# Gate and up of an FFN column tile as one 2x2 block product with seven products for eight

## The chip, the cores and the metric

The kernel runs on one core of a Trainium2 chip. The metric is the device time of one execution in microseconds; the median of three runs is given. The engines are TensorE (PE, and PEld for its weight loads), VectorE (DVE), ScalarE (ACT), GpSimd (POOL) and SyncE (SP), which issues most transfers.

## What is computed

One decoder layer, on 512 prompt tokens and 8 x 4 sample tokens together (T = 544 columns), in float32. Only the two FFNs change; they are the macaron half steps before and after the mixing part:

```
def swiglu(x, w_gate, w_up, w_down):
    return (jax.nn.silu(x @ w_gate) * (x @ w_up)) @ w_down

# per layer, D_MODEL = 1024, D_FF = 2816
x = x + 0.5 * SwiGLU_1(RMSNorm(x))
h = RMSNorm(x); z = h @ w_in          # seven groups of columns
x = x + concat(MoBA(q_a, k_a, v_a), gate * norm(HGRN2(q_b, f_b, i_b))) @ w_out
x = x + 0.5 * SwiGLU_2(RMSNorm(x))
```

## The kernel before

Activations lie feature-major: 8 tiles of 128 features by 544 tokens, and a product is taken in two halves of 272 tokens. Float32 accuracy comes from a split of each operand into two float32r parts, hi and lo; one k tile of a product is three matmuls, hi x hi, hi x lo and lo x hi (`gemm_unit`). ACT makes the high part of a weight (a cast, `whi`), DVE the low one (`wlo` = raw - hi). The moving operands are `xh`, `xl` for the input of an FFN and `hh`, `hl` for its hidden features.

Each FFN has 22 column tiles of 128 hidden features, in groups of 8, 8 and 6 (`FGROUPS`). For each tile `gemm` makes the gate product and then the up product, each of 8 k tiles in two halves, so 96 matmuls of 272 columns. `hidden` evacuates them: gate x R (R is 1/rms per token) into `t_g`, Silu into `t_s`, times R, and up x `t_s` into `t_h`, which is split into `hh` and `hl`. After a group come its eight down products (`ffn`), each of 48 matmuls (36 in the last group), which are added to x.

A weight block is 8 k tiles by 128 columns (512 KB). `w_dma` loads it on SP's queue into one of two raw buffers, `w_split` splits it into one of two pairs `whi`, `wlo`; `next_w` takes a block and starts the split and the load of later ones.

The order of all instructions comes from a planner. `Order.run` steps a backbone of products and several side chains (norms, attention, the recurrence, loads of tables); `Engine.cost` estimates each instruction, and `give_out` writes the instructions out sorted by estimated start. On each engine they then run in that order, so an instruction that waits holds back all behind it. PSUM has eight banks, three of them (`NMM`) for the products, named `mm`.

The planner's estimate of a float32r matmul, and the call that this change replaces for most tiles, are these lines:

```
            if args[1].dtype == F32R:
                self.order.columns = n * rows
                return n / 2400.0 + OVER
...
                yield from self.gemm(xg, KD, gate, both=f == 0)
                yield from self.gemm(xg, KD, up)
```

Of the kernel before, what the change touches and what calls it, by code (L numbers as in the profile page):

```python
# [50 lines left out]
OVER, TICK, WARM_COLUMNS = 0.0027, 3.413, 3060  # L51
# [42 lines left out]
class Root:  # L94
    """A tile that is allocated when the first instruction that uses it is given out."""
# [10 lines left out]
class View:  # L106
    """A view of such a tile; model has the same shape."""
# [30 lines left out]
class Rows:  # L138
    """Row indices of an indirect load."""
# [36 lines left out]
class Engine:  # L176
    """Passes instructions on and keeps an estimate of when each of them runs."""
# [65 lines left out]
class Order:  # L243
    """Writes down the steps of several dependent chains between the units of a backbone of matrix
    products, in the order in which they are expected to be ready, and gives the instructions out
    in the order in which they are expected to start."""
# [40 lines left out]

    def fit(self, part, s, cost):
        """the first time from s on at which the engine is free for so long"""
# [91 lines left out]
class Core:  # L381
    """The engines, each behind an estimate of its time."""
# [9 lines left out]
class Build:  # L392
# [31 lines left out]
    # ---- weights: [nk*128, 128] blocks, each split exactly into two float32r parts, loaded ahead  # L424
    def weight_blocks(self):
        a, out = self.a, []

        def block(m, nk, r0, c0):
            out.append((m[128 * r0:128 * (r0 + nk), c0:c0 + 128].rearrange("(k p) m -> p k m", p=128), nk))

        def ffn(p):
            for g0, ng in FGROUPS:
                for f in range(g0, g0 + ng):
                    block(a[p + "_gate"][0], KD, 0, 128 * f)
                    block(a[p + "_up"][0], KD, 0, 128 * f)
                for m in range(KD):
                    block(a[p + "_down"][0], ng, g0, 128 * m)

        ffn("ffn1")
        for n, j in IN_ORDER:  # L440
            block(a["w_in"][0], KD, 0, COLS[n] + 128 * j)
        for m in range(KD):
            block(a["w_out"][0], KD, 0, 128 * m)
        ffn("ffn2")
        return out

    def w_dma(self):
        if self.w_loaded < len(self.blocks):
            src, nk = self.blocks[self.w_loaded]
            raw = self.tl(self.wp, [128, 8, 128], "raw", bufs=2)  # L450
            self.nc.sync.dma_start(raw[:, :nk], src)
            self.w_raw.append((raw, nk))
            self.w_loaded += 1

    def w_split(self):
        if self.w_raw:
            nc = self.nc
            raw, nk = self.w_raw.pop(0)
            hi = self.tl(self.wp, [128, 8, 128], "whi", F32R, bufs=2)
            lo = self.tl(self.wp, [128, 8, 128], "wlo", F32R, bufs=2)  # L460
            nc.scalar.copy(hi[:, :nk], raw[:, :nk])
            nc.vector.tensor_tensor(lo[:, :nk], raw[:, :nk], hi[:, :nk].bitcast(F32), op=ALU.subtract)
            self.w_ready.append((hi, lo))

    def first_weights(self):
        """the first block, loaded and split by halves: returns it and the steps that load and split"""
        nc = self.nc
        src, nk = self.blocks[self.w_loaded]
        self.w_loaded += 1
        raw = self.tl(self.wp, [128, 8, 128], "raw", bufs=2)  # L470
        hi = self.tl(self.wp, [128, 8, 128], "whi", F32R, bufs=2)
        lo = self.tl(self.wp, [128, 8, 128], "wlo", F32R, bufs=2)
        parts = [slice(i, i + nk // 2) for i in (0, nk // 2)]

        def load(i):
            nc.sync.dma_start(raw[:, parts[i]], src[:, parts[i]])

        def split(i):
            k = parts[i]
            nc.scalar.copy(hi[:, k], raw[:, k])  # L480
            nc.vector.tensor_tensor(lo[:, k], raw[:, k], hi[:, k].bitcast(F32), op=ALU.subtract)

        return (hi, lo), load, split

    def next_w(self, ahead=True):
        if not self.w_ready:
            self.w_split()
            self.w_dma()
        w = self.w_ready.pop(0)
        if ahead and not self.w_ready:  # L490
            self.w_split()
        if len(self.w_raw) < 2:
            self.w_dma()
        return w

    def gemm_unit(self, ps, h, w, k, x, first, last):
        nc = self.nc
        (hi, lo), (xh, xl) = w, x
        for i, (ww, xx) in enumerate(((hi, xh), (hi, xl), (lo, xh))):
            nc.tensor.matmul(ps[:, :HT], ww[:, k], xx[:, self.cols(h)], start=first and i == 0, stop=last and i == 2)  # L500

    def gemm(self, x, nk, evac, order=None, both=False):
        """a product by halves of the tokens, each evacuated when it is done;
        both: the halves side by side, for operands that are just being made"""
        w = self.next_w()
        ks = list(order or range(nk))
        ps = []
        for hh in ((0, 1),) if both else ((0,), (1,)):
# [5 lines left out]
            for n, k in enumerate(ks):  # L514
                for h in hh:
                    self.gemm_unit(ps[h], h, w, k, x[k], n == 0, n == nk - 1)
# [5 lines left out]
            if self.have_R():  # L522
                self.flush()

# [21 lines left out]
    # ---- 1/sqrt(mean + eps) on a small tile  # L546
# [17 lines left out]
    def norm_add(self, m, x):  # L564
        """adds the squares of feature tile m of x to the running sum"""
# [9 lines left out]
    def norm(self):  # L575
        """chain: R = 1/rms per token, over all partitions"""
# [24 lines left out]
    def hidden(self, pool, i, hs):  # L601
        """evacuations of gate and up of one tile of hidden features: silu(gate) * up, split"""
# [12 lines left out]
        def up(p, h):  # L615
            c = self.cols(h)
            nc.vector.tensor_tensor(u[:, c], p, s[:, c], op=ALU.mult)
            if h:
                hi = self.tl(pool, [128, T], f"hh{i}", F32R)
                lo = self.tl(pool, [128, T], f"hl{i}", F32R)  # L620
                nc.scalar.copy(hi, u)
                nc.vector.tensor_tensor(lo, u, hi.bitcast(F32), op=ALU.subtract)
                hs[i] = hi, lo
# [3 lines left out]
    # ---- SwiGLU half step; x: list of feature-major tiles updated in place  # L627
    def ffn(self, pool, x, xg, done, first=None):
        nc = self.nc
        for g0, ng in FGROUPS:  # L630
            hs = {}
            for f in range(g0, g0 + ng):
                gate, up = self.hidden(pool, f - g0, hs)
# [7 lines left out]
            yield from self.settle()  # L641
            for m in range(KD):
# [29 lines left out]
    def small(self, rp):  # L672
        """chain: loads and tables for the middle part, spread over time"""
# [34 lines left out]
        self.rs = rp.tile([HEADS, RLEN], F32, name="rsb")  # L708
# [8 lines left out]
    def small_setup(self):  # L717
        nc = self.nc
        nc.vector.tensor_copy(self.lm, self.lmi)
        # lower bound lb -> (1 - lb) / 2, its complement and its negative  # L720
# [13 lines left out]
        # page table -> row-group indices of every (batch, quarter)  # L734
# [4 lines left out]
        # relative bias per distance, reversed: r[h, y] = bias of distance RTOP - y  # L739
        for c0 in range(0, RLEN, 512):  # L740
# [3 lines left out]
            nc.vector.tensor_copy(self.rs[:, c0:c0 + n], p[:HEADS, :n])  # L744
        rd = self.dp.tile([HEADS, RLEN], F32, name="rbias")
        nc.sync.dma_start(rd, self.rs)
        # one row per query offset, so that skewed reads have a positive step
# [8 lines left out]
    def load_x(self, pool, p, x):  # L756
        """x by column chunks, turned feature-major and split as they come"""
# [15 lines left out]
        self.blocks = self.weight_blocks()  # L773
        self.w_loaded, self.w_raw, self.w_ready = 0, [], []
# [55 lines left out]
        for n in range(KD + LAG):  # L830
# [10 lines left out]
            for m in range(2):  # L841
                k = n - LAG * m
                if 0 <= k < KD:
                    for h in range(2):
                        self.gemm_unit(ps[m][h], h, w[m][0], k, xg[k], k == 0, k == KD - 1)
                if n == 4 and m == 0:
                    self.w_dma()
                    self.w_dma()
                if n == KD - 1 and m == 0:
                    self.w_split()  # L850
# [4 lines left out]
        self.w_split()  # L855
        self.w_dma()
        self.w_dma()
        return xg, out

    def ffn1(self, xspill):  # L860
        nc = self.nc
        with self.pool("ffn1") as pool, self.pool("relb") as rp:
# [6 lines left out]
            out = []  # L869

# [5 lines left out]
            yield from self.ffn(pool, x, xg, done, first)  # L876
# [21 lines left out]
    def stack(self, dst, src, i):  # L898
        """src [NS, 128] split in two parts: the high one twice, the low one as block 1 + i of dst"""
# [10 lines left out]
    def to_tokens(self, z, dst, dst_s):  # L910
        """feature-major [128, T] -> dst [128 tok, 4, 128] and dst_s [NS, 128], or stacked parts of it"""
# [711 lines left out]
```

## Time and profile before

| | |
|---|---|
| Time, median of 3 runs (lowest, highest) | 1244.88 us (1244.19, 1245.5) |
| Span of the profiled execution | 1246.9 us |
| PE busy | 1223.8 us, 98% |
| DVE busy | 672.2 us, 54% |
| ACT busy | 406.5 us, 33% |
| POOL busy | 127.8 us, 10% |
| Mean DMA rate | 116 GB/s |

The profiled execution is shown by its span alone, from its first to its last instruction, 2.0 us above the median of the three runs. The first FFN runs to about 430 us, the mixing part from there to about 800 us, the second FFN from about 843 us to the end. A busy PE says little of itself, since matmuls overlap; what the parts of an FFN cost is read from the number of matmuls in a stretch.

### The profile page before, as it was taken

What the parts mean: (1) busy time and instruction counts of PE and PEld (TensorE: products, weight loads), DVE (VectorE), ACT (ScalarE), POOL (GpSimd) and SP (SyncE); (2) the same over time, 40 slices, a digit from 0 to 9 for tenths busy, and PEclk for the clock granted to TensorE, in tenths of its full rate; (3) what the DMA queues carried; (4) which work ended last, traced back from release to release, by engine and by line L of the source; (5) the groups of instructions that cost most, each with busy time, mean ns of one, the idle gap of its engine ahead of it and who ended that gap; (6) DMA issues with size and microseconds to landing.
All of it is one profiled execution on the core that took longest, in us unless ns stands there. A gap on an engine that the chain in (4) does not pass through costs nothing.

```text
span 1246.9 us, 25516 instructions
## 1 busy us (share of the span) xinstructions
PE 1223.8 (98%) x10979; PEld 1161.4 (93%) x10979; DVE 672.2 (54%) x1309; ACT 406.5 (33%) x685; POOL 127.8 (10%) x143
## 2 busy tenths in 40 slices
PE   8999999999999999999999999899999999999998
PEld 7999999999999998988878876799999999999998
DVE  5544434443445678888667557655443344433443
ACT  5322222221223325555445423332221122212222
POOL 3000000000000231001233244120000000000000
PEclk8999999999999999999999999999999999999999
DMA  5333343323233552332665786332223232332333
GB/s 143 88 87 94 113 144 95 92 86 85 85 92 97 181 179 71 103 91 72 188 188 172 230 270 225 128 96 86 85 85 101 84 88 85 86 94 84 92 87 88
DMA packets 213476, 144.68 MB, mean 116 GB/s; under 512 B 9299, under 2 KB 201323, under 8 KB 213364
## 3 DMA queue, kind: packets, MB, share of 16 engines
q1 hardware_dynamic: 202836, 106.59, 29.4%
q0 software_dynamic: 10432, 36.32, 8.8%
q8 instruction: 87, 1.43, 0.5%
q14 instruction: 25, 0.20, 0.1%
q10 hardware_dynamic: 96, 0.14, 0.0%
HBM read 133.94 MB, written 11.83 MB: 117 GB/s over the span
## 4 chain that ended last, share of the span: by engine, by line
PE 92%; DVE 3%; DMA 2%; ACT 2%; issue 1%; SPq 0%; ACTq 0%
PE mm L273 78%; PE sm L273 15%; DMA raw<-ffn_gate 2%; DVE wlo L273 1%; ACT whi L273 0%; ACT sq L273 0%; DVE sc L273 0%; DVE sst L273 0%; DVE xl L273 0%; ACT SC L273 0%; DVE y_n L273 0%; DVE st L273 0%; DVE hf L273 0%; ACT sc L273 0%; DVE kn L273 0%
## 5 line engine op out<-in xcount | busy, mean ns | idle before, releaser
L273 PE MATMUL mm<-xh,whi 128*128 128x272 f32 x1952 | 576.0, 295 | 5.0 <-ACT xh L273 5.0
L273 PE MATMUL mm<-xh,wlo 128*128 128x272 f32 x1952 | 563.6, 289 | 2.8 <-DVE wlo L273 2.8
L273 PE MATMUL mm<-xl,whi 128*128 128x272 f32 x1952 | 563.2, 289 | 1.7 <-DVE xl L273 1.7
L273 PEld LDWEIGHTS mm<-xh,whi 128*128 128x128 f32 x1952 | 369.5, 189 | 22.8 <-issue 15.9
L273 PEld LDWEIGHTS mm<-xh,wlo 128*128 128x128 f32 x1952 | 368.8, 189 | 3.6 <-DVE wlo L273 3.4
L273 PEld LDWEIGHTS mm<-xl,whi 128*128 128x128 f32 x1952 | 369.2, 189 | 2.9 <-DVE xl L273 2.6
L273 ACT CAST whi<-raw 128x1024 fp32r<-128x1024 f32 (+2 forms) x174 | 176.5, 1015 | 220.4 <-PE mm L273 190.6
L273 DVE TENSOR_TENSOR wlo<-raw,whi 128x1024 fp32r<-128x1024 f32 (+2 forms) x174 | 216.4, 1244 | 55.5 <-ACT whi L273 54.8
L273 PE MATMUL mm<-hh,whi 128*128 128x272 f32 x704 | 203.2, 289 | 0.0
L273 PE MATMUL mm<-hh,wlo 128*128 128x272 f32 x704 | 202.9, 288 | 0.0
L273 PE MATMUL mm<-hl,whi 128*128 128x272 f32 x704 | 202.1, 287 | 0.0
L273 PEld LDWEIGHTS mm<-hh,whi 128*128 128x128 f32 x704 | 132.8, 189 | 0.3 <-issue 0.2
L273 PEld LDWEIGHTS mm<-hh,wlo 128*128 128x128 f32 x704 | 132.4, 188 | 0.0
L273 PEld LDWEIGHTS mm<-hl,whi 128*128 128x128 f32 x704 | 132.2, 188 | 0.0
L273 DVE TENSOR_TENSOR t_g<-mm,R 128x272 f32<-128x272 f32 x86 | 37.6, 438 | 100.1 <-PE mm L273 100.0
L273 DVE TENSOR_TENSOR t_h<-mm,t_s 128x272 f32<-128x272 f32 x86 | 37.5, 437 | 97.6 <-PE mm L273 97.5
L273 ACT CAST hh<-t_h 128x544 fp32r<-128x544 f32 x44 | 28.5, 647 | 187.3 <-DVE t_h L273 187.3
L273 ACT ACTIVATE t_s<-t_g 128x544 f32<-128x544 f32 x44 | 28.9, 658 | 185.1 <-DVE t_g L273 185.1
L273 POOL TENSOR_TENSOR sqsum<-sqsum,sq 128x544 f32<-128x544 f32 x18 | 25.8, 1436 | 419.3 <-ACT sq L273 419.0
L273 DVE SCALAR_TENSOR_TENSOR y<-mm,y 128x272 f32<-128x272 f32 x48 | 21.0, 441 | 72.5 <-PE mm L273 72.5
L273 DVE SCALAR_TENSOR_TENSOR x<-mm,x 128x272 f32<-128x272 f32 x48 | 20.9, 441 | 54.2 <-PE mm L273 54.0
L273 ACT COPY KT<-sm 128x512 f32<-128x512 f32 x64 | 34.4, 588 | 47.4 <-PE sm L273 47.4
(241 smaller groups left out, 1069.6 us busy)
## 6 DMA issues: line engine op xcount, KB each, us to landing
raw<-ffn_gate SPq DMA_DIRECT2D x43, 512.0 KB
raw<-ffn_up SPq DMA_DIRECT2D x43, 512.0 KB
raw<-ffn_down SPq DMA_DIRECT2D x32, 512.0 KB
raw<-w_in SPq DMA_DIRECT2D x28, 512.0 KB
raw<-ffn_down SPq DMA_DIRECT2D x16, 384.0 KB
raw<-w_out SPq DMA_DIRECT2D x8, 512.0 KB
rprompt<-rbias SPq DMA_DIRECT2D x1, 2556.0 KB
xs<-x SPq DMA_DIRECT2D x8, 272.0 KB
```

Of the source, the lines that this page charges most:

```text
L273: call(*map(real, args), **{k: real(v) for k, v in kw.items()})
```

## The change

The first four column tiles of each FFN (`NREG`) stay as they were. From the fifth on, gate and up of a tile are taken as the two row blocks of a 2x2 product: its left factor has the blocks gate and up by the first and the last four k tiles, its right factor these two groups of k tiles by the two halves of the tokens. Strassen's scheme in Winograd's form needs seven products of 4 k tiles instead of eight.

- The left factors are a11, a12, a21, a22 (four loads of 256 KB) and four sums S0 to S3 of them, which POOL makes; seven of these eight are split by ACT and DVE (`w_split`), a unit of 4 k tiles each.
- The right factors are made once for each FFN, as a side chain (`right_factors`): the scaled input (x, gain and R) of two k tiles on DVE, four differences on POOL, and splits on ACT and DVE into seven slices of `xwh` and `xwl`.
- `paired_gemm` takes the seven products one after another, each with one PSUM buffer and one evacuation of 272 columns; `hidden_paired` puts gate and up together from them: two copies on ACT, five additions on DVE with an operand in PSUM, two late additions on POOL (`t_s` and `t_h`, right halves), two Silus of half a tile, one product on DVE.
- All weights are loaded and split in units of 4 k tiles with four raw and four split buffers. In the paired tiles the freed tiles of `xh` and `xl` serve as four more raw and six more split buffers (`more_slots`), so units named `xh`, `xl` there are weights. Loads and splits are started when a unit is released (`free_w`, `w_pump`).
- The table of relative biases goes through a smaller buffer in three pieces, and the planner's constant `OVER` is 0.0112 for 0.0027 us.

The core of the diff:

```
-OVER, TICK, WARM_COLUMNS = 0.0027, 3.413, 3060
+OVER, TICK, WARM_COLUMNS = 0.0112, 3.413, 3060
+NREG = 4
...
+                    if f < NREG:
+                        plain(gate, KD, 0, 128 * f)
+                        plain(up, KD, 0, 128 * f)
+                    else:
+                        out.append({"paired": True, "nk": KD // 2, "raw": [], "done": 0,
+                                    "src": quarters(gate, KD, 0, 128 * f) + quarters(up, KD, 0, 128 * f)})
...
+    def w_split(self):
...
+        if job["paired"]:
+            (a11, a12, a21, a22) = (r for r, _ in job["raw"])
+            if n == 0:
+                S = [self.tl(self.sums, [128, 4, 128], f"S{i}") for i in range(4)]
+                for i, (p, q, op) in enumerate(((a21, a22, ALU.add), (S[0], a11, ALU.subtract),
+                                                (a11, a21, ALU.subtract), (a12, S[1], ALU.subtract))):
+                    self.nc.gpsimd.tensor_tensor(S[i][:, :nk], p[:, :nk], q[:, :nk], op=op)
+                job["units"] = (a11, S[0], S[1], S[2], a12, S[3], a22)
+            src = job["units"][n]
+            self.units.append(self.split_unit(src, nk, x))
...
+    PAIRED = (0, 3, 4, 5, 1, 2, 6)
+
+    def paired_gemm(self, xw, nk, evacs):
...
+        for r, evac in zip(self.PAIRED, evacs):
+            w, = self.next_w(1)
+            ps = self.mm()
+            for k in range(nk):
+                xh, xl = xw[k]
+                self.products(ps, w, k, xh[:, r], xl[:, r], k == 0, k == nk - 1)
+                yield
+            evac(ps[:, :HT])
+            self.free_w([w])
...
+            for B, m in ((B1, k), (B2, k + n)):
+                nc.vector.scalar_tensor_tensor(B.rearrange("p a b -> p (a b)"), x[m],
+                                               self.gains[:, gain, m:m + 1], self.R, op0=ALU.mult, op1=ALU.mult)
+                pace(1.2)
+                yield
+            for out, p, q in ((S1[:, 0], B1[:, 1], B1[:, 0]), (S1[:, 1], B2[:, 1], S1[:, 0]),
+                              (S2[:, 0], B2[:, 1], B1[:, 1]), (S2[:, 1], B2[:, 0], S1[:, 1])):
+                nc.gpsimd.tensor_tensor(out, p, q, op=ALU.subtract)
+            split(hi, lo, slice(0, 1), B1[:, 0:1])
...
+    def hidden_paired(self, pool, i, hs):
...
+        s1, s5, u2, u3 = p[:, l], p[:, r], q[:, l], q[:, r]
+        add = lambda out, x, y: nc.vector.tensor_tensor(out, x, y, op=ALU.add)
+        late = lambda out, x, y: nc.gpsimd.tensor_tensor(out, x, y, op=ALU.add)
+
+        def p6(x):
+            add(u2, x, s1)
+            late(s[:, r], u2, s5)
+
+        def p7(x):
+            add(u3, x, u2)
+            late(u[:, r], u3, s5)
+
+        def p2(x):
+            add(s[:, l], x, s1)
+            nc.scalar.activation(s[:, l], s[:, l], AF.Silu)
+
+        def p3(x):
+            add(s[:, r], x, s[:, r])
+            nc.scalar.activation(s[:, r], s[:, r], AF.Silu)
+
+        def p4(x):
+            add(u[:, l], x, u3)
+            nc.vector.tensor_tensor(u, u, s, op=ALU.mult)
+            hs[i] = self.split_hidden(u, i)
...
+                if f >= NREG:
+                    if f == NREG:
+                        yield from self.settle()
+                        yield lambda: len(self.xw) == KD // 2
+                        self.more_slots(home)
+                        self.w_pump()
+                    yield from self.paired_gemm(self.xw, KD // 2, self.hidden_paired(pool, f - g0, hs))
+                    continue
```

Three places show what it does to the order of the engines. On DVE, one column tile of the first group stands so before (the `wlo` rows split blocks of later products):

```order
L273 TENSOR_TENSOR t_g_97_739<-mm_103_696,R_72_479 128x272
L273 TENSOR_TENSOR t_g_97_739<-mm_104_730,R_72_479 128x272
L273 TENSOR_TENSOR t_s_98_770<-t_s_98_770,R_72_479 128x544
L273 TENSOR_TENSOR wlo_106_789<-raw_92_676,whi_105_776 128x1024
L273 TENSOR_TENSOR t_h_99_802<-mm_108_761,t_s_98_770 128x272
L273 TENSOR_TENSOR t_h_99_802<-mm_109_795,t_s_98_770 128x272
L273 TENSOR_TENSOR hl3_111_844<-t_h_99_802,hh3_110_835 128x544
L273 TENSOR_TENSOR wlo_116_854<-raw_102_742,whi_115_841 128x1024
```

With the change a paired tile in the middle of the second group (the thirteenth, between its first and its last evacuation on DVE) stands so on DVE; `sq1`, `t_s` and `t_h` with an `mm` operand are evacuations, the `xl` and `wlo` rows split units of the next tile and of the one after it:

```order
L274 TENSOR_TENSOR sq1_550_2899<-mm_558_2873,t_g_549_2855 128x272
L274 TENSOR_TENSOR xl6_560_2910<-S3_534_2783,xh6_559_2896 128x512
L274 TENSOR_TENSOR sq1_550_2899<-mm_561_2893,sq1_550_2899 128x272
L274 TENSOR_TENSOR xl7_563_2930<-raw_494_2630,xh7_562_2921 128x512
L274 TENSOR_TENSOR t_s_547_2908<-mm_565_2918,t_g_549_2855 128x272
L274 TENSOR_TENSOR xl2_571_2953<-xh0_502_2651,xh2_570_2945 128x512
L274 TENSOR_TENSOR t_s_547_2908<-mm_572_2942,t_s_547_2908 128x272
L274 TENSOR_TENSOR xl3_574_2974<-S0_566_2827,xh3_573_2966 128x512
L274 TENSOR_TENSOR t_h_548_2928<-mm_575_2963,sq1_550_2899 128x272
L274 TENSOR_TENSOR t_h_548_2928<-t_h_548_2928,t_s_547_2908 128x544
L274 TENSOR_TENSOR xl4_579_3000<-S1_567_2858,xh4_578_2987 128x512
L274 TENSOR_TENSOR hl4_577_3015<-t_h_548_2928,hh4_576_3003 128x544
```

Two more splits follow before the next tile's first evacuation, so seven splits, five evacuations, one product and one `hl` make a tile, and each evacuation but the last has a split behind it. On POOL, which had nothing there before, the same tile's late additions stand among the sums for the tile after the next:

```order
L274 TENSOR_TENSOR S0_566_2827<-xl1_522_2746,raw_529_2785 128x512
L274 TENSOR_TENSOR S1_567_2858<-S0_566_2827,xh0_502_2651 128x512
L274 TENSOR_TENSOR S2_568_2882<-xh0_502_2651,xl1_522_2746 128x512
L274 TENSOR_TENSOR t_s_547_2908<-sq1_550_2899,t_g_549_2855 128x272
L274 TENSOR_TENSOR t_h_548_2928<-sq1_550_2899,t_g_549_2855 128x272
L274 TENSOR_TENSOR S3_569_2938<-xh1_503_2594,S1_567_2858 128x512
```

The fourth evacuation in the piece above (`t_s_547` from `mm_572`) reads what POOL's fourth row writes, and the split from `S0_566` what its first row writes. At the third place, the third tile of the first FFN, the making of the right factors has come between the evacuations and splits on DVE (`hl6` holds a scaled k tile here, `xwl1` is the low part of the right factors):

```order
L274 SCALAR_TENSOR_TENSOR hl6_104_699<-x5_187,gains_141,R_86_507 128x544
L274 TENSOR_TENSOR xwl1_108_709<-hh6_103_644,xwh1_107_656 128x272
L274 TENSOR_TENSOR t_g_117_714<-mm_120_612,R_86_507 128x272
L274 TENSOR_TENSOR xwl1_108_709<-hl6_104_699,xwh1_107_656 128x544
L274 TENSOR_TENSOR t_g_117_714<-mm_121_650,R_86_507 128x272
L274 TENSOR_TENSOR xwl1_108_709<-hh7_105_654,xwh1_107_656 128x544
L274 TENSOR_TENSOR t_s_118_741<-t_s_118_741,R_86_507 128x544
L274 TENSOR_TENSOR xwl1_108_709<-hl7_106_721,xwh1_107_656 128x544
L274 TENSOR_TENSOR wlo_123_767<-raw_99_504,whi_122_677 128x512
```

Between the first use of R and the last evacuation of the fourth tile, DVE has 8 such scalings, 16 splits of right factors, 9 splits of weight units, and the 12 evacuations and 11 further steps of the hidden tiles that were there before.

## Rows read from the trace of the kernel before

**Rows 1.** The page: span, busy times, and the chain by engine

```profile
span 1246.9 us, 25516 instructions
PE 1223.8 (98%) x10979; PEld 1161.4 (93%) x10979; DVE 672.2 (54%) x1309; ACT 406.5 (33%) x685; POOL 127.8 (10%) x143
PE 92%; DVE 3%; DMA 2%; ACT 2%; issue 1%; SPq 0%; ACTq 0%
```

**Rows 2.** Windows: start:end, length; busy us of PE, PEld, DVE, ACT, POOL; clock, DMA

```profile
124.70:200.00 75.30, 74.56 (x583) 72.55 (x582) 30.73 (x57) 17.58 (x19) 0.00 (x0) 1.00 0.40 123
...
300.00:400.00 100.00, 100.00 (x802) 100.00 (x802) 44.48 (x66) 25.96 (x33) 1.37 (x1) 1.00 0.30 89
...
700.00:800.00 100.00, 93.47 (x1326) 72.55 (x1324) 63.93 (x162) 33.29 (x84) 35.24 (x37) 0.98 0.62 199
```

**Rows 3.** The chain in order of time: start, us, what

```profile
47.14 93.78 PE mm L273 x748
...
154.92 13.16 DMA raw<-ffn_gate
...
847.09 360.29 PE mm L273 x2877
```

**Rows 4.** Groups by line, 200 to 400 us: busy us, mean ns, idle before

```profile
L273 DVE TENSOR_TENSOR wlo<-raw,whi 128x1024 fp32r<-128x1024 f32 x30 | 36.7, 1225 | 9.0 <-ACT whi L273 9.0
L273 DVE TENSOR_TENSOR t_h<-mm,t_s 128x272 f32<-128x272 f32 x24 | 10.5, 437 | 28.2 <-PE mm L273 28.1
...
L273 DVE TENSOR_TENSOR hl<-t_h,hh 128x544 fp32r<-128x544 f32 x12 | 8.7, 726 | 8.6 <-ACT hh L273 8.6
L273 DVE TENSOR_TENSOR t_s<-t_s,R 128x544 f32<-128x544 f32 x12 | 8.7, 725 | 8.7 <-ACT t_s L273 8.7
...
L273 ACT ACTIVATE t_s<-t_g 128x544 f32<-128x544 f32 x12 | 7.9, 660 | 54.0 <-DVE t_g L273 54.0
```

**Rows 5.** Views of single tiles: ns of one, least/median/most, and the forms

```profile
L273 DVE TENSOR_TENSOR wlo<-raw,whi x174: 681/1225/2842, 7.9 to 1232.3; 128x1024 fp32r<-128x1024 f32 x154, 128x768 fp32r<-128x768 f32 x16, 128x512 fp32r<-128x512 f32 x4
L273 ACT CAST whi<-raw x174: 611/1045/1080, 6.2 to 1231.4; 128x1024 fp32r<-128x1024 f32 x154, 128x768 fp32r<-128x768 f32 x16, 128x512 fp32r<-128x512 f32 x4
L273 POOL TENSOR_TENSOR sqsum<-sqsum,sq x18: 1357/1368/1738, 18.7 to 834.8; 128x544 f32<-128x544 f32 x18
L273 PE MATMUL mm<-hl,whi x704: 282/287/292, 119.1 to 1241.2; 128*128 128x272 f32 x176
```

**Rows 6.** Timeline of DVE and POOL, 20 to 27 us: start, us, instruction

```profile
20.58 1.84 DVE L273 TENSOR_TENSOR wlo<-raw,whi 128x512 fp32r<-128x512 f32 x1
22.34 0.77 DVE L273 SCALAR_TENSOR_TENSOR xl<-x,gains,xh 128x544 fp32r<-128x544 f32 x1
23.04 0.68 DVE L273 COPY x<-sm 128x512 f32<-128x512 f32 x1
23.64 1.29 DVE L273 SCALAR_TENSOR_TENSOR xl<-x,gains,xh 128x544 fp32r<-128x544 f32 x1
24.86 1.88 DVE L273 SCALAR_TENSOR_TENSOR xl<-x,gains,xh 128x544 fp32r<-128x544 f32 x1
...
20.44 1.43 POOL L273 TENSOR_TENSOR sqsum<-sqsum,sq 128x544 f32<-128x544 f32 x1 [0.37 <-ACT sq L273]
...
24.43 1.73 POOL L273 TENSOR_TENSOR sqsum<-sqsum,sq 128x544 f32<-128x544 f32 x1
```

**Rows 7.** Where R comes and its FFN begins: timeline of DVE, chain in time

```profile
39.04 0.69 DVE L273 COPY R<-sm 128x512 f32<-128x512 f32 x1 [1.31 <-PE sm L273]
846.90 0.69 DVE L273 COPY R<-sm 128x512 f32<-128x512 f32 x1 [1.30 <-PE sm L273]
...
31.20 2.81 PE mm L273 x21
34.00 1.11 PE sm L273 x10
...
842.99 2.99 PE mm L273 x24
```

More of the change, by code (lines that the diff above doesn't have):

```diff
@@ L455, in w_split, with room @@
-    def w_split(self):
[L456 to L463, printed above, removed]
-    def first_weights(self):
[L467 to L473, printed above, removed]
+    def room(self, kind, job):
+        free = [x for x in self.slots[kind] if x["used"] < x["bufs"] and (x["extra"] is None or job["paired"])]
+        if not free:
+            return None
+        x = min(free, key=lambda x: x["freed"][0] if len(x["freed"]) else -1.0)
+        x["used"] += 1
+        if x["freed"]:
+            x["freed"].pop(0)
+        return x
@@ new lines, in release, with more_slots @@
+    def release(self, x, *tiles):
+        x["used"] -= 1
+        x["freed"].append(self.order.free["pe"])
+        self.order.done.update(t.name for t in tiles)
+    def more_slots(self, pool):
+        for i in range(KD):
+            if i < 2:
+                for t in ("xh", "xl"):
+                    self.slots["raw"].append({"pool": pool, "tags": (f"{t}{i}",), "bufs": 1, "used": 0, "freed": [],
+                                              "extra": pool})
+            else:
+                self.slots["w"].append({"pool": pool, "tags": (f"xh{i}", f"xl{i}"), "bufs": 1, "used": 0,
+                                        "freed": [], "extra": pool})
@@ new lines, in w_pump, with next_w, free_w @@
+    def w_pump(self):
+        while self.w_split() or self.w_load():
+            pass
+    def next_w(self, n):
+        if len(self.units) < n:
+            self.w_pump()
+        w, self.units = self.units[:n], self.units[n:]
+        assert len(w) == n
+        return w
+    def free_w(self, w, pump=True):
+        for hi, lo, x in w:
+            self.release(x, hi, lo)
+        if pump:
+            self.w_pump()
+    def first_weights(self):
+        job = self.jobs[self.loading]
+        self.loading += 1
+        self.splitting += 1
+        rs = [self.room("raw", job) for _ in range(2)]
+        ws = [self.room("w", job) for _ in range(2)]
+        raws = [self.take_slot(x, (F32,))[0] for x in rs]
+        w = []
@@ L475, in load @@
         def load(i):
-            nc.sync.dma_start(raw[:, parts[i]], src[:, parts[i]])
+            self.nc.sync.dma_start(raws[i], job["src"][i])
         def split(i):
[L479 to L494, printed above, removed]
@@ L496, in gemm_unit, with products @@
-    def gemm_unit(self, ps, h, w, k, x, first, last):
-        nc = self.nc
-        (hi, lo), (xh, xl) = w, x
+            w.append(self.split_unit(raws[i], 4, ws[i]))
+            self.release(rs[i], raws[i])
+        return w, load, split
+    def products(self, ps, w, k, xh, xl, first, last):
+        hi, lo, _ = w
         for i, (ww, xx) in enumerate(((hi, xh), (hi, xl), (lo, xh))):
-            nc.tensor.matmul(ps[:, :HT], ww[:, k], xx[:, self.cols(h)], start=first and i == 0, stop=last and i == 2)
+            self.nc.tensor.matmul(ps[:, :HT], ww[:, k], xx, start=first and i == 0, stop=last and i == 2)
@@ L707, in small @@
         load(self.oh, a["onehot"])
-        self.rs = rp.tile([HEADS, RLEN], F32, name="rsb")
+        self.rs = lambda: self.tl(rp, [HEADS, 512], "rsb")
         for dst, src in loads:
```

177 lines of the change are left out of this document (136 added, 41 removed).

## The prediction

> **What bounds the kernel now.** The busy times and the chain of waits come first: TensorE is busy for 1223.8 of 1246.9 us, and it makes up 92% of the chain [rows 1]. A stage split by windows shows where that holds: in the FFN stretches PE is busy for 100.00 of 100 us at granted clock 1.00, DVE for 44, POOL for 1; in the middle part PE is at 93 [rows 2]. So an FFN stretch costs what its matmuls cost, as long as DVE (evacuations and the low halves of the weights) keeps up. The price of one matmul comes from long unbroken pieces of the chain: 2877 in 360.29 us and 748 in 93.78 us, 125.2 and 125.4 ns [rows 3]. The 287 ns that a single one is shown to last [rows 5] overlap with its neighbours and are no price.
>
> **What the change removes.** A regular column tile is 96 matmuls of 272 columns, a paired one 7 x 4 x 3 = 84. There are 18 paired tiles in each FFN, so 36 x 12 = 432 fewer; at 125.2 ns a tile takes 10.52 for 12.02 us, and the sum is **-54.1 us**. The Trainium skill ("TensorE: Matmul & The Clock Gate", section "Wait — 56ns, not 53.3ns?") gives columns over 2.4 GHz plus about 2.5 ns, 115.8 ns here; no row shows that, the trace has 125.2, and by the page's figure the estimate would be -50.0 us. Loads stay at 1 MB per tile; halving the transfers adds some 0.4 us of SP issue each, which nothing waits for at one group of four per 10 us.
>
> **What it adds on DVE and POOL, per paired tile.** DVE before: two splits of 1024 (1.225 each), four evacuations (0.44), t_s x R and hl (0.725 each): 5.7 of 12.02 us [rows 4]. After, as the order of DVE shows: seven splits of 512 (0.68, the least time shown for that width [rows 5]), five evacuations (0.44), one product and one hl: 8.4 us, of 10.52. ACT gets seven casts of 0.61 [rows 5], two copies from PSUM and two Silus of half a tile (each under the 0.66 of a whole one [rows 4]) and a cast: 7.6 us at most, not the limit. POOL, idle here before, gets four sums of 512 and two of 272. Its nearest row is the 128x544 add, 1.37 us alone [rows 5]; by width 1.29 and 0.68, or 6.5 us.
>
> Each of the three alone fits into 10.52 us. DVE and POOL together may not. Between 20 and 27 us both work on SBUF pairs, and they wait for each other [rows 6]. The split of 512 that is issued at 20.58, during POOL's add (20.44 to 21.87), takes 1.84 for 0.68 and ends 0.55 after POOL. POOL's add at 24.43 ends 1.23 after DVE's (24.93), and DVE's next one, issued at 24.86, ends 0.58 after POOL (26.16). The copy from PSUM at 23.04 runs beside POOL in its usual 0.68. So instructions with two SBUF operands exclude one another on the two engines, and an evacuation (one operand in PSUM) does not take part. I price the excluded stretch at 0.55 to 0.62 for a DVE split, 0.6 for a 544 one, 1.16 (1.23 x 512/544) and 0.62 for POOL's. A paired tile then holds 7 x 0.57 + 2 x 0.6 + 4 x 1.16 + 2 x 0.62 = **11.1 us** of mutually exclusive work against 10.52 us of matmuls, provided that all five evacuations hide behind POOL. With none hidden (each follows the one before 0.08 sooner than its length, 0.36 [rows 6]) it is 12.9. The order puts a POOL sum or late add beside every evacuation, so I take 11.1 to 11.4: about 0.7 us per tile more than PE needs.
>
> What is late next: in DVE's order a split stands between two evacuations, for a weight unit nine products ahead. So the buffers of split weights cannot absorb a slow DVE; an evacuation that is late can, by three PSUM buffers, two products of 1.50 less one evacuation: 2.6 us per run of paired tiles. After a run come eight down products with 48 matmuls each (36 in the last), where DVE catches up.
>
> **Right factors.** They run on DVE, ACT and POOL while the regular tiles still do. In the first FFN, R is copied at 39.0 and the second tile's matmuls began at 31.2 [rows 7]; three regular tiles (288 x 0.1252 = 36.1 us) and the norm's two groups of matmuls (some 1.2 each) let PE reach tile 4 at 69.7. DVE has by then, from R to the last evacuation of tile 3, 8 scalings (0.70), 19 of 544 (0.65), 8 of 272 (0.36), 9 splits (0.61), 12 evacuations (0.36) and the copy of R: 31.3 us, so 70.3 without any wait. Waits for ACT are put at 2 us. POOL's 16 differences and two sums exclude 12.2 us, of which 4 hide behind evacuations. That makes 80.5: DVE is about 10 us late. Tiles 4 to 7 then hold 33 splits (nine units are built up), 7 others, 18 sums, 8 late adds: 18.8 + 4.2 + 20.9 + 5.0 = 48.9 against 42.1 us, 7 more. Less 2.6 that gives **+14 us**. In the second FFN a whole further tile stands ahead (its matmuls begin at 843.0, R at 846.9 [rows 7]), so the right factors end about a tile ahead of need; there only tiles 4 to 7 count, 6.8 less 2.6, taken as **+5**. Tiles 8 to 15: 8 x 0.58 to 0.88, 4.6 to 7.0 less 2.6, about 4 in each FFN, **+8**. Tiles 16 to 21 have no following pair to split: 0. At the table of biases, where one transfer took 13.16 us and PE lost about 2 us (583 matmuls in 75.3 us are 73.0 us of work) [rows 2, 3], the tenth tile's units now come behind the same transfer: 0, with 0 to +4 in the range. The planner's constant for a matmul (0.116 to 0.1245 us) reorders the middle part too; its PE idle there, 6.5 us in the worst window [rows 2], bounds it: 0, within -5 to +6.
>
> **Sum.** 1246.9 - 54.1 + 14 + 5 + 8 = 1219.8 us of span. The profiled span is 2.0 above the median of the runs (1244.88), so the time should be **1218 us**.
>
> **The rivals.** *Light:* POOL's work falls under evacuations and DVE's idle 2 us per tile, and only the start of the first FFN costs 5 to 9: 1196 to 1200, up to 1208 with part of the rest. For it: 44% DVE load before. Against: rows 6, where nothing overlapped. *Heavy:* half of the evacuations are not hidden, 12.0 us per tile: 36 x 1.48 = 53 less 6 x 2.6, plus 10 for the first start: 48, so 1239. *Slower:* the exclusion covers whole instructions, start-up included: 7 x 0.68 + 2 x 0.725 + 4 x 1.29 + 2 x 0.68 = 12.7 us per tile. That is 36 x 2.2 = 79, less 15.6, plus 10: 73 us of waits against 54.1 saved, 1264. It decides from 12.1 us per tile. For it: the 1.84 us; against: 0.55 of the split's 0.68 and 1.23 of the add's 1.37 are what is excluded. "SBUF — State Buffer" of the Trainium skill ("Who interferes with whom") says just this: a DVE instruction with two SBUF inputs and a GpSimd one that reads SBUF block each other for the whole instruction. The trace agrees on the block, less on its length. *Transfers:* weights late behind the 2.5 MB table, +4: inside the range. That the work is not removed is excluded: the order of PE has 432 rows fewer.
>
> **How the numbers follow.** Forecast (waits of 17 to 40 us, 1208 to 1231) 0.55; light 0.15; heavy (1231 to 1242) 0.12; within 0.2% (2.5 us, about what a measurement can tell from no change) 0.05; slower 0.13. Faster 0.82. The range 1202 to 1243 leaves out the slower case and half of the light one.
>
> **What would show it.** PE 432 matmuls fewer at 125 ns; in tiles 9 to 14 windows of 10.5 us should hold fewer than 84 matmuls, some 76 to 80, with DVE and POOL together near full. Splits of 512 should last 0.7 to 1.9 us, many over 1.2, POOL's sums 1.3 to 1.75. PE's longest waits should name DVE, at 70 to 90 us above all, and the clock stay 1.00. I am wrong if PE waits neither there nor in tiles 8 to 15, if a split keeps 0.7 beside POOL, or if the waits name a transfer.

## The result, and the profile after

The changed kernel takes 1228.66 us in the median of four runs (1228.14 to 1230.7), the kernel before 1244.54 on the same chip (the three runs above and one more): a ratio of 0.9876, with a 95% interval of 0.9857 to 0.9895. It is 15.9 us faster. The time forecast was 1218, the range 1202 to 1243. Seen in the profiles, the span went from 1246.9 [rows 1] to 1227.3 us, 19.6 less.

The page of the changed kernel, with its span and busy times:

```profile
span 1227.3 us, 26588 instructions
PE 1184.0 (96%) x10547; PEld 1114.1 (91%) x10547; DVE 911.0 (74%) x1671; ACT 544.0 (44%) x1103; POOL 473.3 (39%) x391
```

Against [rows 1] PE has the 432 matmuls fewer, and DVE is busy for 911 us where it was 672. The page's mean of 74% hides where: the windows of the changed kernel over its six stretches of paired tiles (tiles 4 to 7, 8 to 15 and 16 to 21 of the first and of the second FFN), with the columns of [rows 2]:

```profile
73.16:127.65 54.49, 46.77 (x338) 44.99 (x337) 51.32 (x63) 27.93 (x54) 40.71 (x28) 0.94 0.44 119
177.89:269.83 91.94, 87.35 (x674) 84.80 (x673) 86.53 (x110) 48.68 (x97) 69.01 (x48) 1.00 0.34 98
317.83:382.43 64.60, 64.20 (x507) 63.29 (x505) 55.52 (x77) 32.47 (x66) 39.62 (x28) 1.00 0.23 66
883.83:933.32 49.49, 44.70 (x338) 43.72 (x337) 46.91 (x60) 26.77 (x52) 35.30 (x25) 0.97 0.46 132
981.33:1069.58 88.25, 86.37 (x674) 84.64 (x673) 84.46 (x109) 47.18 (x95) 64.03 (x44) 1.00 0.34 96
1117.59:1182.17 64.58, 64.09 (x507) 63.35 (x505) 55.40 (x77) 32.43 (x66) 39.02 (x28) 1.00 0.23 66
```

A stretch of four paired tiles is 336 matmuls, 42.1 us at 125.2 ns; one of eight is 84.1, one of six 63.1. What the row's length has beyond that is waiting: 12.4, 7.8, 1.5, 7.4, 4.1 and 1.5 us. In the first two groups of each FFN DVE is 94 to 96% busy, in the last ones 86%. PE is shown at 86 to 99%, so its busy share alone hides part of the waiting (4.6 of the 7.8 us of the second row show); the number of matmuls in a row shows it. The down products behind each stretch run at 125.0 to 125.2 ns as before, but for those of the first group of the first FFN, which lose 2.2 us, in before as well. PE's longest waits in the changed kernel (engine and what it waited for: us in total, times, longest) name DVE's evacuations and splits first, ACT's copies out of PSUM third, and among those of the products (`mm`) no transfer:

```profile
PE mm L274 <- DVE sq L274: 9.3, 8, 3.1
PE mm L274 <- DVE wlo L274: 8.1, 8, 1.9
PE mm L274 <- ACT t_g L274: 5.7, 9, 2.1
PE mm L274 <- DVE xl L274: 4.9, 3, 3.6
PE sm L274 <- DMA KV<-cache_v,idx: 1.4, 2, 1.0
```

One tile of the second group, from its first evacuation to the next tile's, in the timeline of DVE and then of POOL (start, us, instruction):

```profile
210.23 0.43 DVE L274 TENSOR_TENSOR sq<-mm,t_g 128x272 f32<-128x272 f32 x1
210.58 1.41 DVE L274 TENSOR_TENSOR wlo<-S,whi 128x512 fp32r<-128x512 f32 x1
211.91 0.43 DVE L274 TENSOR_TENSOR sq<-mm,sq 128x272 f32<-128x272 f32 x1
212.26 0.91 DVE L274 TENSOR_TENSOR wlo<-raw,whi 128x512 fp32r<-128x512 f32 x1
213.10 0.43 DVE L274 TENSOR_TENSOR t_s<-mm,t_g 128x272 f32<-128x272 f32 x1
213.45 0.90 DVE L274 TENSOR_TENSOR wlo<-xh,whi 128x512 fp32r<-128x512 f32 x1
214.28 0.43 DVE L274 TENSOR_TENSOR t_s<-mm,t_s 128x272 f32<-128x272 f32 x1
214.63 1.43 DVE L274 TENSOR_TENSOR wlo<-S,whi 128x512 fp32r<-128x512 f32 x1
215.98 0.43 DVE L274 TENSOR_TENSOR t_h<-mm,sq 128x272 f32<-128x272 f32 x1
...
221.72 0.43 DVE L274 TENSOR_TENSOR sq<-mm,t_g 128x272 f32<-128x272 f32 x1
```

```profile
209.78 1.66 POOL L274 TENSOR_TENSOR S<-xh,xh 128x512 f32<-128x512 f32 x1 [0.62 <-DVE xl L274]
211.40 1.23 POOL L274 TENSOR_TENSOR t_s<-sq,t_g 128x272 f32<-128x272 f32 x1
212.59 1.22 POOL L274 TENSOR_TENSOR t_h<-sq,t_g 128x272 f32<-128x272 f32 x1
213.76 1.74 POOL L274 TENSOR_TENSOR S<-xl,S 128x512 f32<-128x512 f32 x1
216.18 1.28 POOL L274 TENSOR_TENSOR S<-xl,raw 128x512 f32<-128x512 f32 x1 [0.67 <-DVE wlo L274]
```

The tile takes 221.72 - 210.23 = 11.49 us where its matmuls need 10.52. DVE is hardly ever idle, but the four splits of 512 shown last 0.90 to 1.43 us, beside a POOL instruction, for 0.68 alone, and its evacuations 0.43 always. Four of the five evacuations lie inside a POOL instruction (210.23, 211.91, 213.10 and 214.28); the fifth, at 215.98, begins while POOL is idle. Over tiles 8 to 15 of both FFNs it is 61 of 78 evacuations. The 11.49 us are also the mean of the first FFN's second group (91.94 / 8); in the second FFN it is 11.03 (88.25 / 8).

### The profile page after: what moved, and what is told of

It is laid out like the page before. It is cut to its first block, busy times and chain, and to the rows that moved or that the text cites. A ratio compares the mean times of both kernels' runs of the same rounds, so it can differ in the third digit from the quotient of the medians.

```text
span 1227.3 us, 26588 instructions
## 1 busy us (share of the span) xinstructions
PE 1184.0 (96%) x10547; PEld 1114.1 (91%) x10547; DVE 911.0 (74%) x1671; ACT 544.0 (44%) x1103; POOL 473.3 (39%) x391
## 5 line engine op out<-in xcount | busy, mean ns | idle before, releaser
L274 PE MATMUL mm<-xh,whi 128*128 128x272 f32 x1152 | 346.4, 301 | 1.5 <-ACT xh L274 1.0
L274 PE MATMUL mm<-xh,wlo 128*128 128x272 f32 x1152 | 334.1, 290 | 5.0 <-DVE wlo L274 5.0
L274 PE MATMUL mm<-xl,whi 128*128 128x272 f32 x1152 | 333.9, 290 | 5.0 <-DVE xl L274 4.9
L274 PEld LDWEIGHTS mm<-xh,whi 128*128 128x128 f32 x1152 | 218.8, 190 | 18.7 <-issue 16.0
L274 DVE TENSOR_TENSOR wlo<-raw,whi 128x512 fp32r<-128x512 f32 (+1 forms) x224 | 172.0, 775 | 73.5 <-ACT whi L274 69.7
L274 PEld LDWEIGHTS mm<-xl,whi 128*128 128x128 f32 x1152 | 219.3, 190 | 6.2 <-DVE xl L274 6.1
L274 PEld LDWEIGHTS mm<-xh,wlo 128*128 128x128 f32 x1152 | 218.9, 190 | 6.1 <-DVE wlo L274 6.1
L274 PE MATMUL mm<-xwh,xh 128*128 128x272 f32 x624 | 184.3, 295 | 10.8 <-DVE sq L274 7.8
L274 PE MATMUL mm<-xwl,xh 128*128 128x272 f32 x624 | 181.4, 291 | 0.0
L274 PE MATMUL mm<-xwh,xl 128*128 128x272 f32 x624 | 181.4, 291 | 0.0
```

Of the source, the lines that this page charges most:

```text
L274: call(*map(real, args), **{k: real(v) for k, v in kw.items()})
```

## The experiments

Each run is compared with the kernel before by a ratio of runs on one chip. Four of them (sums on DVE, sums and differences on DVE, pairs from the ninth tile, the planner's constant) ran on a chip where the kernel before takes 1250.47 us, so their times stand 6 to 7 us higher and only the ratios are carried over.

**No sums.** The sums and their tiles are gone, and the units are split from raw blocks:

```
-                S = [self.tl(self.sums, [128, 4, 128], f"S{i}") for i in range(4)]
-                for i, (p, q, op) in enumerate(((a21, a22, ALU.add), (S[0], a11, ALU.subtract),
-                                                (a11, a21, ALU.subtract), (a12, S[1], ALU.subtract))):
-                    self.nc.gpsimd.tensor_tensor(S[i][:, :nk], p[:, :nk], q[:, :nk], op=op)
-                job["units"] = (a11, S[0], S[1], S[2], a12, S[3], a22)
+                job["units"] = (a11, a12, a22, a12, a12, a22, a22)
```

> Leaves out POOL's four sums per paired tile: the raw blocks a11, a12, a22 are split seven times in their place, so casts, splits, evacuations and matmuls stay as many. Exclusion (DVE and POOL instructions with two SBUF operands block each other): a paired tile then holds 7 x 0.57 + 2 x 0.6 + 2 x 1.1 = 7.4 us of exclusive work under 10.52 us of matmuls, so the waits of tiles 8 to 21 go (about 14 us over both FFNs) and most of those of tiles 4 to 7 (10 to 15 of 20): 1199 to 1207 us. DVE's own work and order: DVE does exactly what it did, so 1224 to 1230 us. Dependence (splits that wait until POOL's sums are written): as with the exclusion, 1199 to 1207 us; the next kernel tells the two apart.

Measured: 1198.08 us, ratio 0.9645 (0.9619 to 0.9672), 1 us under the range of exclusion. The windows over tiles 4 to 7 and 8 to 15 of the first FFN show it:

```profile
71.85:116.97 45.12, 42.94 (x338) 42.21 (x337) 39.46 (x67) 28.36 (x55) 10.13 (x9) 1.00 0.55 146
169.01:253.03 84.02, 84.02 (x675) 84.02 (x674) 64.18 (x109) 50.49 (x96) 20.32 (x16) 1.00 0.36 104
```

PE no longer waits in tiles 8 to 15 (84.02 us for 84.1 of work), and 3.1 us are left in tiles 4 to 7. DVE does 109 instructions in 64.2 us there, for 110 in 86.5 in the changed kernel; its splits last 0.69 us in the mean there, for 1.12. Its own work is therefore not what PE waited for.

**Sums that nothing reads.** POOL makes the sums as in the changed kernel, and only the line of `job["units"]` is the one above.

> POOL makes the four sums of each paired tile as in the changed kernel, but nothing reads them: the units are split from a11, a12, a22 as in the kernel without sums. Exclusion: POOL blocks DVE as before, so the waits stay, 1222 to 1231 us, and DVE's splits keep their lengths up to 1.8 us. Dependence: splits no longer wait for a sum, so it falls to the time without sums, 1199 to 1207 us. DVE's own work: 1224 to 1230 us.

Measured: 1233.24 us, ratio 0.9914 (0.9892 to 0.9936), 2 us over the range of exclusion and far from that of dependence. The sums alone, which no split waits for, cost 1233.24 - 1198.08 = 35 us on the same chip. In the windows of the same two stretches DVE is as full as in the changed kernel:

```profile
73.12:127.92 54.80, 46.63 (x338) 45.72 (x337) 53.46 (x64) 26.64 (x53) 41.22 (x28) 0.91 0.43 118
179.73:271.49 91.76, 86.04 (x674) 84.48 (x673) 87.42 (x110) 48.35 (x96) 64.11 (x46) 1.00 0.35 101
```

So dependence on the sums falls as an explanation, and the blocking of one engine by the other is shown. Nor is it the late additions that come late: in the whole of the changed kernel DVE is idle for 2.2 us waiting for POOL, and here for 1.9. It is even 4.6 us slower than the changed kernel, spread over the paired stretches and the first group's down products. In tiles 8 to 15 of both FFNs 45 of 78 evacuations lie inside a POOL instruction, for 61, which would work that way; no run shows that it is the cause.

**Late additions on DVE.**

```
-        late = lambda out, x, y: nc.gpsimd.tensor_tensor(out, x, y, op=ALU.add)
+        late = lambda out, x, y: nc.vector.tensor_tensor(out, x, y, op=ALU.add)
```

> The two late additions of 272 of each paired tile are made on DVE in place of POOL, nothing else. Exclusion: two POOL instructions of 1.10 us each become two DVE ones of 0.36, so a tile's exclusive work falls from 11.5 to about 10.1 us, under the 10.52 us of its matmuls; tiles 8 to 21 lose most of their 14 us of waits and tiles 4 to 7 some 4 to 8: 1206 to 1214 us. DVE's own work: 72 more instructions of 0.36 us on the engine that is behind, 26 us more work: 1232 to 1250 us. Dependence: an evacuation no longer waits for POOL, 1218 to 1226 us.

Measured: 1252.27 us, ratio 1.0068 (1.0051 to 1.0086): 24 us slower than the changed kernel, where my account expected 15 to 22 less. A tile of the second group of the first FFN takes 97.48 / 8 = 12.2 us (in the second FFN 11.6). The timeline of this kernel, DVE and then POOL, at the same place in a tile:

```profile
214.88 0.43 DVE L274 TENSOR_TENSOR sq<-mm,t_g 128x272 f32<-128x272 f32 x1
215.34 1.06 DVE L274 TENSOR_TENSOR t_s<-sq,t_g 128x272 f32<-128x272 f32 x1
...
216.93 0.43 DVE L274 TENSOR_TENSOR sq<-mm,sq 128x272 f32<-128x272 f32 x1
217.39 1.32 DVE L274 TENSOR_TENSOR t_h<-sq,t_g 128x272 f32<-128x272 f32 x1
218.64 0.68 DVE L274 TENSOR_TENSOR wlo<-raw,whi 128x512 fp32r<-128x512 f32 x1
219.24 0.43 DVE L274 TENSOR_TENSOR t_s<-mm,t_g 128x272 f32<-128x272 f32 x1
```

```profile
214.43 1.67 POOL L274 TENSOR_TENSOR S<-xh,xh 128x512 f32<-128x512 f32 x1 [0.63 <-DVE xl L274]
217.14 1.27 POOL L274 TENSOR_TENSOR S<-xl,S 128x512 f32<-128x512 f32 x1 [1.04 <-issue]
```

POOL's next sum begins at 222.50, so of the tile's five evacuations (214.88, 216.93, 219.24, 220.19, 221.28) only the first lies inside a POOL instruction; over tiles 8 to 15 of both FFNs it is 16 of 78. Two things in my expectation were wrong. I took a late addition on POOL at 1.10 us, its whole length where it begins behind a split of DVE's; but the split beside it lasts 0.91 for 0.68, so with the evacuation that it hides it blocks DVE for about 0.6, as the prediction had priced it. And I left out the hiding. With the prediction's own prices a tile now has 11.1 - 2 x 0.62 + 2 x 0.36 = 10.6 us of exclusive work and four open evacuations of 0.36, 12.0 us for the 12.2 measured. The same sum gives the changed kernel 11.1 + 0.36 = 11.5, as measured. In the second FFN both kernels take about 0.5 us per tile less than this sum.

**That again without the sums**, as a test of this account: the edits of the first and the third kernel together.

> Leaves out POOL's four sums (units split from a11, a12, a22, as in the first kernel of the study) and makes the two late additions on DVE. Moving them cost 24 us while POOL made sums. If that was POOL's sums, which then fell beside two-operand work of DVE and no longer beside evacuations (a tile took 12.2 us, which is 10.5 of exclusive work and 5 unhidden evacuations of 0.36), the move costs nothing without them: ratio to the kernel before 0.962 to 0.967, as without sums alone (0.9645). If it was DVE's own added work and its order, the 24 us come back: ratio 0.975 to 0.985.

Measured: 1197.77 us, ratio 0.9628 (0.9607 to 0.9649). The 24 us are not DVE's 72 instructions: without POOL's sums they cost nothing. In the window of tiles 8 to 15 DVE is busy for 69 of 84 us, and PE is not held up:

```profile
168.94:252.97 84.03, 84.03 (x674) 84.03 (x673) 69.32 (x125) 50.02 (x96) 0.00 (x0) 1.00 0.36 103
```

**Units of 4 k tiles alone.** `NREG = 22`, and no right factors are spawned.

> Units of 4 k tiles with four raw and four split buffers alone: no tile is paired and no right factors are made (all 22 tiles are regular). My account of the change gives this part nothing: 1243 to 1247 us, as the kernel before, with the first matmul about 1.2 us later and the middle part about 1.2 us shorter. Rival: finer units feed TensorE better, or their 0.68 us splits and 256 KB loads cost something of their own: 1236 to 1241, or over 1249.

Measured: 1241.05 us, ratio 0.9977 (0.9966 to 0.9988), some 2.9 us faster by itself: not the nothing of my account, and at the edge of the first rival. In the profile its fifth tile begins at 67.35 us, against 70.99 before. Of these 3.6 us, 2.3 are there after the first 96 matmuls (28.72 for 31.04); the rest comes mostly between 40 and 47 us, where the chain of before goes over ACT's cast and DVE's split of a whole block:

```profile
39.90 1.05 ACT whi L273
...
45.87 1.23 DVE wlo L273
```

and the chain of this kernel has one unbroken piece:

```profile
36.38 93.00 PE mm L274 x744
```

**Sums on DVE.** `nc.vector` in place of `nc.gpsimd` in the loop over the sums.

> The four sums of each paired tile are made on DVE in place of POOL; the two late additions stay on POOL. Exclusion: four sums cost DVE 0.60 each in place of blocking it for 1.16 each; a tile on DVE is then 11 x 0.60 + 2 x 0.65 + 5 x 0.36 = 9.7 us plus some 0.25 from each late addition, 10.2 of 10.52: the waits of tiles 8 to 21 go (some 14 us), those of tiles 4 to 7 shrink by 5 to 10 us: 1203 to 1212 us. Rival, DVE as the bound: moving the late additions there cost 24 us, since DVE then had nothing of POOL's to hide evacuations behind and works in order; 144 more instructions of 0.68 us, which also wait for landing blocks with evacuations queued behind, then cost 10 us or more: 1235 to 1260 us.

Measured: ratio 0.9721 (0.9697 to 0.9744), 1215.52 us beside 1250.47, which on the chip of the changed kernel would be 0.9721 x 1244.54 = 1209.8: the first account. The waits of tiles 8 to 21 are 1.6 us in all for 14.9. Those of tiles 4 to 7 shrank less than it said, to 10.7 and 5.2 from 12.4 and 7.4.

**Sums and differences on DVE.** Also the differences in `right_factors`.

> As the kernel before in this list, and also the 16 differences of the right factors of each FFN on DVE (0.36 us each) in place of POOL (1.1 us each). Exclusion: 16 differences block DVE for some 8 us net in the first FFN and cost 5.8 on DVE, so 1 to 4 us less than with the sums alone: 1200 to 1210 us. DVE as the bound: 2 to 6 us more than with the sums alone.

Measured: ratio 0.9691 (0.9672 to 0.971), 1211.72 us beside 1250.47. It has the lowest ratio of the kernels that leave nothing out, 1.9% under the changed one (0.9691 / 0.9876), but its interval overlaps those of the kernel just before it and of the one with pairs from the ninth and the fifth tile (0.972). Tiles 4 to 7 and 8 to 15 of the first FFN and 4 to 7 of the second:

```profile
71.68:123.03 51.35, 45.68 (x338) 44.80 (x337) 48.04 (x84) 29.55 (x57) 9.06 (x8) 0.93 0.48 129
173.67:258.33 84.66, 84.66 (x674) 84.46 (x673) 77.67 (x135) 50.34 (x96) 18.62 (x16) 1.00 0.34 99
874.76:921.09 46.33, 42.63 (x338) 42.16 (x337) 42.62 (x74) 27.51 (x53) 9.11 (x8) 1.00 0.47 136
```

Four sums on DVE take less of its time than they blocked when POOL made them: 135 instructions in 77.7 us, for 110 in 86.5. The 9.3 and 4.3 us that stay in tiles 4 to 7 are DVE's own: the next kernel, which has nothing left on POOL there, keeps 9.3 and 3.9.

**Everything on DVE**, the late additions too.

> Sums, late additions and the differences of the right factors all on DVE; POOL does nothing in the paired tiles. A tile on DVE is 11 x 0.60 + 2 x 0.65 + 7 x 0.36 = 10.4 us, just under its 10.52 us of matmuls, with nothing of POOL's to wait for. Exclusion with hiding: 0 to 10 us more than with the late additions on POOL, ratio 0.969 to 0.977. DVE's order as the cause of the 24 us: ratio 0.985 to 0.99.

Measured: 1213.58 us, ratio 0.976 (0.9739 to 0.9781), inside the first account. DVE is at 81.67 of 86.47 us in tiles 8 to 15, and PE waits 2.3 us there, for 0.5 with the late additions on POOL: 1.8 us over 16 additions, 0.11 each. That is as the 0.36 for 0.25 of the expectations would have it, though DVE's busy time rises by 4.0 us (81.67 for 77.67).

**Pairs from the ninth tile.** `NREG = 8`.

> Pairs from the ninth tile on (14 tiles of each FFN in place of 18), all else as in the changed kernel. 8 x 12 matmuls come back: +12.0 us. If the waits at tile 4 and in tiles 4 to 7 come from building the right factors and nine units of lookahead beside short tiles, they go, since the down products of the first group now lie ahead of the first pair: -5.8 (start, against the kernel with units alone), -12.4 and -7.4 us: 1213 to 1218 us. If every start of pairing costs that, wherever it is, they move to tile 8: 1230 to 1241 us.

Measured: ratio 0.9853 (0.9834 to 0.9873), beside 0.9876 for the changed kernel: neither account. Four fewer pairs in each FFN lose 12.0 us together and save as much or a little more. The waits of tiles 4 to 7 go (1.1 and 0.0 us for 12.4 and 7.4), but tiles 8 to 15 now have 13.4 and 7.9 for 7.8 and 4.1, and the first eight tiles still take 5.6 us longer than with units alone. So about half of what was lost in tiles 4 to 7 (9.4 of 19.8 us) moves with the start; it fits the building of the lookahead, which is needed wherever pairs begin.

**The planner's constant alone.** `OVER` back at 0.0027.

> The planner's constant for a matmul back at 0.0027 us, all else as in the changed kernel; only the order of instructions changes. My account gives it nothing, with the middle part 0 to 2 us longer: 1227 to 1232 us. Rival: with a matmul costed 7% too short the planner places DVE's and POOL's work of the paired tiles at the wrong products, and evacuations are queued behind splits: 1233 to 1245 us.

Measured: ratio 0.9883 (0.986 to 0.9906), no difference from the changed kernel that this shows. Inside it the waits move: tile 4 begins at 67.52, but tiles 4 to 7 then take 61.30 us, waiting for right factors that are late (for DVE's `xwl` 5.7 us in all, for ACT's `xwh` 4.7).

**Pairs from the ninth tile of the first FFN and the fifth of the second**, with sums and differences on DVE.

> Sums and differences on DVE as in the second kernel of the last list (ratio 0.9691), and the first FFN pairs from its ninth tile on, the second from its fifth. Four pairs fewer: +6.0 us. Of the first FFN's waits at and in tiles 4 to 7 (4.3 and 9.3 us in that run) all go, and 2 to 5 come back in tiles 8 to 15 as the lookahead is built there: -9 to -11. Ratio 0.964 to 0.968. Rival: the lookahead costs as much at tile 8 as at tile 4: 0.970 to 0.975.

Measured: 1208.09 us, ratio 0.972 (0.9701 to 0.9738), the rival's number, but not for its reason. Tiles 8 to 15 have 4.3 us of waits, inside what I gave them; what I had wrong is that the right factors cost PE 5.5 us even among regular tiles (109.36 us for the first eight, 103.90 with units alone).

**The same, right factors at half the pace.** `pace(2.4)` for `pace(1.2)`.

> As the last kernel, with the steps of the right factors at least 2.4 us of TensorE time apart in place of 1.2. With a whole group of tiles and its down products ahead of the first pair, the slower pace lets evacuations pass between the steps in the first FFN: 0 to 3 us less than the last kernel, ratio 0.962 to 0.967; in the second FFN, which still pairs from the fifth tile, the factors may come too late, up to 6 us more.

Measured: 1211.27 us, ratio 0.9739 (0.972 to 0.9759), outside the 0.962 to 0.967 expected. Both halves of the expectation show, in size larger than it had them: windows of the first eight tiles, and of tiles 4 to 7 of the second FFN:

```profile
11.20:114.95 103.75, 102.04 (x806) 101.28 (x805) 79.81 (x148) 49.02 (x86) 9.57 (x7) 1.00 0.36 99
865.93:920.25 54.32, 45.04 (x338) 43.98 (x337) 50.88 (x90) 30.46 (x60) 9.11 (x8) 0.91 0.41 117
```

At this pace the right factors cost nothing among the first eight tiles of the first FFN (103.75 us, for 103.90 with units alone), though the down products behind them wait 4.5 us for 2.9. In the second FFN they come too late, 12.3 us of waits for 4.0, where I had said up to 6 us more. Each pace in the FFN that it suits would be some 4 to 5 us better than either kernel by these rows; it was not run.

## Why the prediction was right, and where it was off

**What bounds it, and what is removed.** 432 matmuls at 125.2 ns: shown by the count, and by down products and undisturbed paired stretches at 125.0 to 125.2 ns.

**DVE against POOL.** The step that carried the forecast, mutual exclusion, is shown by the two kernels with the sums gone (1198.08) and idle (1233.24). "SBUF — State Buffer" of the Trainium skill ("Who interferes with whom") says that a VectorE instruction with two SBUF inputs contends with a GpSimd one that reads SBUF; these two runs agree, with 35 us for 144 sums. In the first FFN its price was right to about 0.1 us: 11.1 us with all evacuations hidden, 11.4 to 11.5 with one open, and 11.49 measured; the kernel with the late additions on DVE gave 12.2 for 12.0. In the second FFN it was about 0.5 too high (11.03 and 11.6), more than the 2.6 us of PSUM buffers, 0.3 per tile, take up; why was not found. POOL's addition of 272 lasts 0.76 us where DVE is idle, not far from the 0.68 I scaled by width; the 1.1 to 1.2 us elsewhere are with the blocking:

```profile
190.03 0.76 POOL L274 TENSOR_TENSOR t_s<-sq,t_g 128x272 f32<-128x272 f32 x1
```

**Where the waits were mis-sized.** The mechanism stood; the terms of the sum did not all. Tiles 8 to 15 were +8 (the 0.58 to 0.88 per tile give 2.0 to 4.4 in each FFN, and I took the upper end) and measured 7.8 + 4.1 - 0.9 (already waited before, in the first FFN) = 11.0: 8 x 0.97 is 7.8, so in the first FFN none of the 2.6 us that I let the three PSUM buffers take up was there, in the second more than that. Tiles 16 to 21 were 0 and measured 1.5 + 1.5: only the last tile has no successor to split, and I had counted all six as if they had none. The second FFN's start was +5 and measured 7.4. The first FFN's start was +14, and against before it measured 2.2 (tile 4 begins at 73.16 for 70.99) and 12.4, or 14.6. That agreement is two misses that cancel: I gave the finer units nothing, and they bring tile 4 to 67.35, so right factors and lookahead, with the lower clock told of below, cost 5.8 + 12.4 = 18.2. The middle part from the first FFN's end to tile 4 of the second was 0 and measured -1.2. That too is two differences: up to the second FFN's first product (838.67 us before by the count of matmuls, not the 843.0 that I read) it is 4.0 us shorter, and tiles 0 to 3 there take 2.8 longer. With units alone tiles 1 to 3 lose nothing, and with right factors at half the pace nothing either, so the right factors cost PE 2.6 us there, a term that I put at nothing because they end ahead of need. Whether the 4.0 us belong to the change is open, since the profiled execution of before seems to have been a long one (below). Together 14.6 + 7.4 + 11.0 + 3.0 - 1.2 = 34.8 us for the 27 forecast: 1246.9 - 54.1 + 34.8 = 1227.6, and the span is 1227.3.

**From span to time.** The last step failed by itself. I took 2.0 us off since the profiled span of before lay 2.0 above the median. In the profiled execution of after, and in those of all twelve experiments, the time lies 1.7 to 2.6 us above the span of that same execution. If the same holds for before, its profiled execution took close to 1249 us, some 4 above its median; the 2.0 belonged on top of the span, and the 4 off the base. Of the 10.7 us between 1218 and 1228.66, 7.5 are the span (1227.3 for 1219.8), so the waits, and some 3 this step. Where that execution lost its 4 us was not found.

**The rivals.** Light is excluded by the windows of the changed kernel; it is what the kernel without sums shows (1198.08, forecast 1196 to 1200 for it). Heavy did not come in the changed kernel, but it is the kernel with the late additions moved: 12.2 us per tile in the first FFN (11.6 in the second) for its 12.0, and slower than before, since its starts (15.5 and 10.9 us) and last groups (5.0 and 4.7) cost more too. The table of biases did not hold the weights up: the waits name no transfer for a product.

**What it should have shown.** Splits of 0.7 to 1.9 us, sums of 1.3 to 1.75 (up to 1.87), DVE near full and PE's waits naming DVE: all there. The clock did not stay at 1.00 everywhere: tiles 4 to 7 show 0.94 and 0.97. The granted clock falls to its lower level (0.50, 1.2 GHz) once in each, after PE had made 73 matmuls in 17.3 us, with its longest wait of 3.1 us among them, and 62 in 12.1:

```profile
90.42:97.25 6.83, 6.03 (x27) 5.70 (x26) 5.78 (x10) 2.10 (x4) 5.43 (x4) 0.50 0.31 83
895.96:899.38 3.42, 3.22 (x14) 3.22 (x15) 3.13 (x7) 0.77 (x2) 3.13 (x3) 0.50 0.35 100
```

The matmuls there follow one another at 0.227 us for 0.125, so the lower clock is at most 27 x 0.10 = 2.7 us of the 12.4 and 1.4 of the 7.4, a term that the forecast had at nothing.

## What to carry to other kernels

Work given to an idle engine is not free when it shares a path with the engine that is nearly full: cost it by what it blocks, and see what it lies beside, since by the prices that fitted the first FFN a POOL addition next to an evacuation from PSUM costs DVE 0.25 us and the four sums next to two-operand work of DVE some 1.16 each, twice what DVE needs to make them itself. A scheme that saves matmuls pays at its start: right factors, lookahead and the lower clock cost more up to the end of tile 7 of the first FFN (18.2 us) than the four pairs there save (6.0), and about half of what tiles 4 to 7 lose moves along when pairs begin later. And a forecast made against a profiled span needs that same execution's time, not the median beside it.

## What was not expected of the hardware

That two engines could be slower with less work between them: moving 72 additions from POOL (some 1.2 us each there) to DVE (0.44 each where nothing blocks) cost 24 us. With them gone one evacuation in five lay inside a POOL instruction, and four in five before (16 and 61 of 78), and without POOL's sums the move cost nothing. Moving POOL's sums and differences too gave all of it back and more (ratio 0.976).
